# A seven-product pair at the end of the last unit of two feed-forward phases

## The chip, the core and the metric

The kernel runs on one core of one Trainium2 chip. The core has a matrix engine (TensorE, PE in the profile), whose stationary operand is loaded by a separate instruction (PEld), a vector engine (DVE), a scalar engine (ACT), a general engine (POOL) and a queue that issues the DMA transfers (SP). Matrix products are summed in eight banks of PSUM, each 128 partitions by 512 float32 values; everything else lies in SBUF. The metric is the device time of one execution in microseconds (us), the median of several runs; lower is better.

## The reference, cut to what matters

Two post-norm layers over 256 tokens of width 2048, each a mixer followed by a SwiGLU feed-forward with 5632 hidden channels:

```python
def swiglu(x, w_gate, w_up, w_down):
    return (jax.nn.silu(x @ w_gate) * (x @ w_up)) @ w_down

    for layer in range(DEPTH):
        ...
        x = layer_norm(DN_ALPHA * x + y, ln_mix_g[layer], ln_mix_b[layer])
        f = swiglu(x, ffn_w_gate[layer], ffn_w_up[layer], ffn_w_down[layer])
        x = layer_norm(DN_ALPHA * x + f, ln_ffn_g[layer], ln_ffn_b[layer])
```

The change lies in `x @ w_gate` and `x @ w_up`, in both layers. Inputs and weights are float32.

## The kernel before

**Products.** A float32 product is made of three matmuls: each operand is split into a rounded high part and the rest, and `mm3` (line 289) adds low x high, high x high and high x low into one PSUM bank. The left operand, 128 tokens by 128 channels, is the stationary one; a weight piece of 128 x 512 streams. Weights come from memory as float32, so every piece that arrives is split first: ACT copies the high part (line 127), DVE subtracts (line 128). A "half" is a transfer of two such pieces into `raw` (`load_half`, line 144, 128 x 1024 in float32, four buffers), split into `whi` and `wlo` (four buffers each in these phases), and it feeds two pieces x two token tiles x three = 12 matmuls.

**Units.** The hidden width is cut into 11 chunks of 512, which `PHASES` (line 67) groups as 3, 4 and 4. In the second and third phase each chunk is one `unit` (line 455). A unit makes four sums, gate and up for both token tiles: `c11` and `c21` are gate, `c12` and `c22` are up. The 16 slices of 128 input channels are taken as eight pairs, in an order that `PAIRS_FIRST`, `PAIRS` or `PAIRS_LAST` gives for the first, the middle and the last unit of a phase. A **plain pair** is two halves: 2 x 2 x 2 products of three matmuls, 24 matmuls. A **seven pair** treats the 2 x 2 blocks (two token tiles and two channel slices, gate and up) by a Winograd scheme with seven products instead of eight: 21 matmuls. Pairs 5, 6 and 7 (`SEVEN`) may be taken so; for them `forms_of` (line 405) makes four combinations of the activations per pair, once for each layer, ahead of the second phase and for all three pairs.

A seven pair's weights come by `load_seven` (line 433): one transfer of 1 MB into `rs`, which has a single buffer; DVE forms four sums of weights `z` (lines 445 to 447, a single buffer too), and seven pieces are split in two goes into `sh` and `sl` (two buffers each): the first three straight from `rs` (lines 444 and 448), the other four from `z` (lines 127 and 128). The seven products of a pair run in this order, each named with the bank it adds to:

```python
SEVEN_ORDER = ((0, "11", "p1"), (5, "f", "p6"), (3, "e", "p5"), (4, "g", "p7"),
               (1, "12", "c11"), (2, "h", "c12"), (6, "22", "c21"))
```

So four further banks, p1, p6, p5 and p7, collect products over a unit's seven pairs. With the four c banks they fill all eight: c on one side (`aside` or `bside` in the profile), p on the other, and the sides swap after every unit. A p bank is opened at a unit's first seven pair and closed by its last.

**The end of a unit** (lines 483 to 501). ACT copies p1 (line 485); DVE forms w, v and x from p6, p5 and p7 (lines 486 to 489), adds w to c21, subtracts v and x from c12 and c22, adds p1 to c11 (490 to 495); ACT takes the SiLU twice (491, 494) and DVE multiplies gate by up (499). Two transposes on PE for each unit (`transpose4`, line 270), one per token tile, are put off by the list `later`, until two and three halves of what comes next have been issued; ACT and DVE then split their result into `yTh` and `yTl`, the left operand of the down projection.

**The end of a phase** (lines 567 to 581). The down projection of the phase's four chunks follows its last unit: four output blocks `n`, each of eight halves, two for each chunk in order, so that the last chunk's `yT` is first read by the seventh half. Its sums start in the banks that held p1 and p6 of the last unit. After the third phase the banks are dealt out anew, as `acc`, `tr` and `mx` (`open_banks("uses")`), over the same memory.

**Order.** The program is not run in the order of this text: a scheduler places the instructions of every engine by priority and by a simulated timeline, and each engine, and SP's queue, then works its list in that order. Weight loads have priority 400, a unit's end 1000. A unit's last products may thus stand among the first products of the next unit.

Of the kernel before, what the change touches and what calls it, by code (L numbers as in the profile page):

```python
# [71 lines left out]
SEVEN = (5, 6, 7)  # L72
# [8 lines left out]
def trunk(ctx: ExitStack, tc: tile.TileContext, a, out):  # L81
# [9 lines left out]
    def open_banks(kind):  # L91

        if banks:
            banks["stack"].close()
        stack = ctx.enter_context(ExitStack())
        pool = stack.enter_context(tc.tile_pool(name="ps", bufs=1, space=PSUM, reuse_waits="tile"))
        banks.update(stack=stack, pool=pool, kind=kind, side=0)
# [16 lines left out]
    def acc():  # L114
        return bank("acc", 3) if banks["kind"] == "uses" else side_bank()
# [4 lines left out]
    def mxp():  # L120
        return bank("mx", 3)
# [15 lines left out]
    def open_ring(pool, bufs):  # L137

        rings.append((pool, bufs))
        turn[0] = -12  # L140
# [37 lines left out]
    def two(k):  # L178
        return k, k + 1
# [72 lines left out]
    def new_xT():  # L252
        xh = [ap_.tile([P, KT, P], F32R, tag=f"xTh{t}", name=f"xTh{t}") for t in range(NT)]
        xl = [ap_.tile([P, KT, P], F32R, tag=f"xTl{t}", name=f"xTl{t}") for t in range(NT)]
        return xh, xl

    def new_yT():
        yh = ap_.tile([P, 4, T], F32R, tag="yTh", name="yTh", bufs=4)
        yl = ap_.tile([P, 4, T], F32R, tag="yTl", name="yTl", bufs=4)
        return yh, yl  # L260

    def x_lhs(xT):
        return lambda tok, k: (xT[0][tok][:, k, :], xT[1][tok][:, k, :])
# [10 lines left out]
    def transpose4(src, hi, lo, ahead_by=0):  # L274
        t = trp()
        for k in range(4):
            transpose(t[:, k * P : (k + 1) * P], src[:, k * P : (k + 1) * P], ident)
        v = t.rearrange("p (k t) -> p k t", k=4)
        with tc.high_priority(offset=ahead_by):
            split(hi, lo, v)  # L280
# [19 lines left out]
    def new_stats():  # L300
        return [sm.tile([P, 4, 6], F32, tag=f"st{t}", name=f"st{t}", bufs=1) for t in range(NT)]
# [79 lines left out]
    def load_gb(pool, i, which):  # L381
        g = pool.tile([P, D], F32, tag="gam", name="gam", bufs=1)
        b = pool.tile([P, D], F32, tag="bet", name="bet", bufs=1)
        nc.sync.dma_start(g, a[f"ln_{which}_g"][i : i + 1, :].to_broadcast([P, D]))
        nc.sync.dma_start(b, a[f"ln_{which}_b"][i : i + 1, :].to_broadcast([P, D]))
        bT = pool.tile([P, 64], F32, tag="betT", name="betT", bufs=1)[:, :KT]
        nc.sync.dma_start(bT, a[f"ln_{which}_bT"][i])
        return g, b, bT
# [20 lines left out]
    def forms_of(sp, xT, out):  # L409

        n = len(SEVEN)
        xs = sp.tile([P, NT, 2 * n, P], F32, tag="rs", name="xs", bufs=1)
        fs = sp.tile([P, 4, n, P], F32, tag="z", name="fs", bufs=1)
        yield
        for t in range(NT):
            s = slice(2 * SEVEN[0], 2 * SEVEN[0] + 2 * n)
            nc.vector.tensor_tensor(xs[:, t], xT[0][t][:, s, :].bitcast(F32), xT[1][t][:, s, :].bitcast(F32), op=add)
            yield
        x11, x12, x21, x22 = (xs[:, t, e : 2 * n : 2, :] for t in range(2) for e in range(2))
        e, f, g, h = (fs[:, i] for i in range(4))  # L420
        nc.vector.tensor_tensor(e, x22, x21, op=sub)
        nc.vector.tensor_tensor(f, e, x11, op=add)
        yield
        nc.vector.tensor_tensor(g, x11, x21, op=sub)
        nc.vector.tensor_tensor(h, x12, f, op=sub)
        yield
        hi, lo = split_tile(sp, [P, 4, n, P], fs, "fm")
        for i, p in enumerate(SEVEN):
            x = lambda t, k: (xT[0][t][:, k, :], xT[1][t][:, k, :])
            e, f, g, h = (at((hi, lo), slice(None), j, i) for j in range(4))  # L430
            out[p] = {"11": x(0, 2 * p), "12": x(0, 2 * p + 1), "22": x(1, 2 * p + 1), "e": e, "f": f, "g": g, "h": h}
# [71 lines left out]
    def ffn(layer, xT, res, mix_pool, close_mix, keep, last):  # L503
        lhs = x_lhs(xT)
        w = a[f"gu{layer}"]

        def whole(c, pool, first):

            gouts = [acc() for _ in range(NT)]
            sil = {}  # L510

            def silu(tok):
                sil[tok] = pool.tile([P, NCH], F32, tag="sil", name="sil", bufs=3)
                nc.scalar.activation(sil[tok], gouts[tok], AF.Silu)

            mm_chunk([(w[c, i][:, :2], (2 * i, 2 * i + 1)) for i in range(8)], lhs, gouts, tok_major=first, after=silu)

            uouts = [mxp() for _ in range(NT)]
            y = new_yT()

            def gated(tok):
                with tc.high_priority(offset=1000):
                    nc.vector.tensor_tensor(sil[tok], sil[tok], uouts[tok], op=mult)
                s = slice(tok * P, (tok + 1) * P)
                later.append([(2 if c == PHASES[0][-1] else 4) + tok, lambda: transpose4(sil[tok], y[0][:, :, s], y[1][:, :, s])])

            mm_chunk([(w[c, i][:, 2:], (2 * i + 1, 2 * i)) for i in range(8)], lhs, uouts, after=gated)
            return y

        stack = ExitStack()  # L530
        forms, making = {}, []

        def make():
            with tc.issue_after(low[-1]):
                if next(making[0], "end") is None:
                    later.append([3, make])

        nxt = cdp = None
        groups = {}
        for pi, chunks in enumerate(PHASES):  # L540
            end = pi == len(PHASES) - 1
            for c in chunks:
                if pi == 0:
                    groups[c] = whole(c, mix_pool, c == 0)
                else:
                    groups[c] = new_yT()
                    pairs = PAIRS_FIRST if c == chunks[0] else PAIRS_LAST if c == chunks[-1] else PAIRS
                    sevens = SEVEN[:-1] if c == chunks[-1] else SEVEN
                    unit(sp, pairs, sevens, w[c], lhs, forms, groups[c], c == chunks[0])
            if pi == 0:  # L550
                close_mix()
                sp = later_pool(stack, f"sp{layer}")
                open_banks("sides")
                making.append(forms_of(sp, xT, forms))
                later.append([2, make])
            gl = [groups[c] for c in chunks]
            if end:
                stack.close()
                open_banks("uses")
                cdp = None if last else keep("cdc")  # L560
                open_ring(keep(f"er{layer}"), 4)
                open_ring(later_pool(stack, f"e{layer}"), 3)
                fp = later_pool(stack, f"g{layer}")
                nxt = None if last else new_xT()
            stats = new_stats()
            evac, norm = residual_tools(res, None, None, None, stats)
            for n in range(4):
                if cdp and n == 1:
                    consts.extend(cd_constants(cdp))
                if end and n == 1:  # L570
                    evac, norm = residual_tools(res, *load_gb(fp, layer, "ffn"), stats)
                outs = [acc() for _ in range(NT)]
                halves = [(a[f"down{layer}"][n, 2 * c + i], two(4 * ci + 2 * i)) for ci, c in enumerate(chunks) for i in range(2)]

                def after(tok):
                    with tc.high_priority(offset=1000 if end and n == 3 else 0):
                        evac(tok, n, outs[tok], pi == 0, end)
                        if end and n == 3:
                            norm(tok, nxt, out if last else None)

                mm_chunk(halves, y_lhs(gl), outs, tok_major=(end and n == 3), after=after)
            if not end:
                banks["side"] ^= 1
        if end:
            rings.pop()
            stack.close()
        return nxt
# [428 lines left out]
    def later_pool(stack, name):  # L1016
        return stack.enter_context(tc.tile_pool(name=name, bufs=1, reuse_waits="tile"))
# [4 lines left out]
    def keep(name):  # L1022
        return later_pool(kept, name)
# [136 lines left out]
```

## Time and profile before

| | |
|---|---|
| median of 3 runs | 2192.04 us (2191.01 to 2192.64) |
| the profiled execution | 2190.72 us, span of its instructions 2188.9 us |
| granted TensorE clock, mean | 0.998 |
| busy: PE, PEld, DVE, ACT | 2170.7, 1804.7, 1558.8 and 1051.3 us |
| matmuls and transposes on PE | 10048 |

The first layer's second and third phase lie between about 655 and 1230 us of the span, the second layer's between about 1603 and 2181 us. A busy PE is not by itself PE at its peak, since a matmul's record is longer than the distance to the next one: the distance of two starts is the measure used here. Times in tables are counted from the first instruction of the span.

### The profile page before, as it was taken

The page shows a single profiled execution, that of the slowest core. Times are in us where ns is not written, and L with a number is a line of the kernel's source. Part 1 is how long each engine was busy: PE and PEld are TensorE (multiplying, and loading weights), DVE is VectorE, ACT ScalarE, POOL GpSimd, SP SyncE. Part 2 cuts the span into 40 slices and gives each one's busy share as a digit, 9 for nine tenths or more (in the row PEclk, how much of TensorE's full clock was granted, in tenths as well). Part 3 has the DMA queues.
Part 4 walks back from the last instruction along what each step waited for, and adds up shares of the span by engine and source line. Part 5 has one row for each costly group of instructions (what it writes and reads, how often), then busy time and mean ns, then how long its engine had stood idle before and what let it go on. Part 6 is the DMA issues. An engine that isn't in the chain of part 4 may idle for free.

```text
span 2188.9 us, 26626 instructions
## 1 busy us (share of the span) xinstructions
PE 2170.7 (99%) x10048; PEld 1804.7 (82%) x10048; DVE 1558.8 (71%) x1954; ACT 1051.3 (48%) x1278; POOL 51.7 (2%) x51
## 2 busy tenths in 40 slices
PE   9999999999999999999999999999999999999997
PEld 7888888888888888888888888888888888888886
DVE  6886688577537787577876776667367896768765
ACT  6445544545435455444545554455344554445442
POOL 0000000000000000000000300000000000000000
PEclk9999999999999999999999999999999999999999
DMA  8555546584736565565549553747456555655563
GB/s 294 161 164 180 167 132 190 195 287 138 237 125 219 188 208 189 189 230 185 199 157 305 165 190 106 235 150 253 143 187 232 185 187 188 222 173 200 172 238 122
DMA packets 112850, 420.64 MB, mean 192 GB/s; under 512 B 13776, under 2 KB 16848, under 8 KB 105808
## 3 DMA queue, kind: packets, MB, share of 16 engines
q1 hardware_dynamic: 112720, 418.93, 57.8%
q8 instruction: 79, 1.29, 0.2%
q14 instruction: 51, 0.42, 0.1%
HBM read 416.78 MB, written 2.10 MB: 191 GB/s over the span
## 4 chain that ended last, share of the span: by engine, by line
PE 96%; DMA 1%; DVE 1%; ACT 0%; issue 0%; SPq 0%; DVEq 0%; ACTq 0%
PE acc L292 41%; PE bside L292 23%; PE aside L292 21%; PE mx L292 7%; PE mx L729 1%; PE tr L124 1%; DMA raw<-in_down 1%; DVE wlo L128 0%; DMA rs<-in_gu 0%; PE mx L775 0%; DMA raw<-in_ab_in 0%; PE bside L124 0%; PE aside L124 0%; PE mx L985 0%; ACT whi L127 0%
## 5 line engine op out<-in xcount | busy, mean ns | idle before, releaser
L128 DVE TENSOR_TENSOR wlo<-raw,whi 128x1024 fp32r<-128x1024 f32 (+1 forms) x673 | 817.8, 1224 | 438.2 <-ACT whi L127 431.2
L127 ACT CAST whi<-raw 128x1024 fp32r<-128x1024 f32 (+1 forms) x673 | 703.7, 1052 | 820.5 <-PE acc L292 262.3
L292 PE MATMUL acc<-whi,xTl 128*128 128x512 f32 x864 | 342.8, 397 | 4.8 <-ACT whi L127 4.8
L292 PE MATMUL acc<-whi,xTh 128*128 128x512 f32 x864 | 340.0, 393 | 0.0
L292 PE MATMUL acc<-wlo,xTh 128*128 128x512 f32 x864 | 337.9, 393 | 0.1
L292 PE MATMUL acc<-whi,yTl 128*128 128x512 f32 x512 | 200.8, 392 | 0.2
L292 PE MATMUL acc<-whi,yTh 128*128 128x512 f32 x512 | 199.6, 390 | 0.0
L292 PE MATMUL acc<-wlo,yTh 128*128 128x512 f32 x512 | 197.7, 390 | 0.0
L292 PEld LDWEIGHTS acc<-whi,xTl 128*128 128x128 f32 x864 | 162.9, 189 | 37.2 <-ACT whi L127 5.7
L292 PEld LDWEIGHTS acc<-wlo,xTh 128*128 128x128 f32 x864 | 162.9, 189 | 33.9 <-DVE wlo L128 1.1
L292 PEld LDWEIGHTS acc<-whi,xTh 128*128 128x128 f32 x864 | 163.1, 189 | 31.1
L292 PE MATMUL bside<-whi,xTl 128*128 128x512 f32 x336 | 131.4, 391 | 0.7 <-ACT g L485 0.6
L292 PE MATMUL bside<-whi,xTh 128*128 128x512 f32 x336 | 131.0, 390 | 0.0
L292 PE MATMUL aside<-whi,xTl 128*128 128x512 f32 x336 | 131.0, 390 | 0.0
L292 PE MATMUL aside<-whi,xTh 128*128 128x512 f32 x336 | 130.9, 390 | 0.0
L292 PE MATMUL bside<-wlo,xTh 128*128 128x512 f32 x336 | 128.1, 390 | 0.0
L292 PE MATMUL aside<-wlo,xTh 128*128 128x512 f32 x336 | 128.1, 390 | 0.0
L292 PEld LDWEIGHTS acc<-wlo,yTh 128*128 128x128 f32 x512 | 96.1, 188 | 20.6 <-DVE wlo L128 0.5
L292 PEld LDWEIGHTS acc<-whi,yTl 128*128 128x128 f32 x512 | 96.2, 188 | 20.0 <-DVE res L310 0.5
L292 PEld LDWEIGHTS acc<-whi,yTh 128*128 128x128 f32 x512 | 96.2, 188 | 19.4
L128 DVE TENSOR_TENSOR sl<-z,sh 128x2048 fp32r<-128x2048 f32 x44 | 100.7, 2289 | 6.4 <-ACT sh L127 5.7
L292 PE MATMUL bside<-whi,yTl 128*128 128x512 f32 x256 | 99.8, 390 | 0.0
(266 smaller groups left out, 3414.3 us busy)
## 6 DMA issues: line engine op xcount, KB each, us to landing
raw<-in_gu SPq DMA_DIRECT2D x264, 512.0 KB, 4.7
raw<-in_down SPq DMA_DIRECT2D x176, 512.0 KB, 3.9
raw<-in_ab_in SPq DMA_DIRECT2D x127, 512.0 KB, 4.2
rs<-in_gu SPq DMA_DIRECT2D x44, 1024.0 KB, 5.9
raw<-in_cd_in SPq DMA_DIRECT2D x40, 512.0 KB, 4.2
raw<-in_ab_out SPq DMA_DIRECT2D x32, 512.0 KB, 4.4
raw<-in_cd_out SPq DMA_DIRECT2D x32, 512.0 KB, 4.2
bias<-in_na_bias SPq DMA_DIRECT2D x32, 64.0 KB, 4.2
```

Source lines behind the costliest of these rows:

```text
L124: return nc.tensor.transpose(o, src, eye)
L127: nc.scalar.copy(hi, src)
L128: return nc.vector.tensor_tensor(lo, src, hi.bitcast(F32), op=sub).ins
L292: ins = nc.tensor.matmul(o, lhs[a], rhs[b], start=start and n == 0, stop=stop and n == 2)
L729: nc.tensor.matmul(m[:, 2 * h + s, :], kk[:, h, s * P : (s + 1) * P], qq[:, h, r * P : (r + 1) * P], start=True, stop=True,)
```

## The change

In each phase's last unit, `sevens` was `SEVEN[:-1]`: pairs 5 and 6 were seven pairs, and pair 7, which is the last in `PAIRS_LAST`, was a plain one. Now pair 7 is a seven pair there too. `PAIRS_LAST` itself, (0, 1, 5, 2, 6, 3, 4, 7), stays. Four units are affected, the last of the second and of the third phase in each of the two layers.

```diff
--- before
+++ after
@@ -545,7 +545,7 @@
                 else:
                     groups[c] = new_yT()
                     pairs = PAIRS_FIRST if c == chunks[0] else PAIRS_LAST if c == chunks[-1] else PAIRS
-                    sevens = SEVEN[:-1] if c == chunks[-1] else SEVEN
+                    sevens = SEVEN
                     unit(sp, pairs, sevens, w[c], lhs, forms, groups[c], c == chunks[0])
```

In `unit`, the following is what the pair then runs through, on the first branch instead of the second:

```python
            if p in sevens:
                ...
                wt = load_seven(sp, w[p], behind.pop(0))
                for i, x, name in SEVEN_ORDER:
                    product(name, forms[p][x], wt(i))
            else:
                for n, ks in ((0, (2 * p, 2 * p + 1)), (1, (2 * p + 1, 2 * p))):
                    hi, lo = load_half(w[p][:, 2 * n : 2 * n + 2])
                    ...
                    half_done()
```

## The prediction, made before the changed kernel was run

> **What bounds the kernel now.** I read the page first: busy times, granted clock, and the chain that ended last.
>
> ```profile
> span 2188.9 us, 26626 instructions
> PE 2170.7 (99%) x10048; PEld 1804.7 (82%) x10048; DVE 1558.8 (71%) x1954; ACT 1051.3 (48%) x1278; POOL 51.7 (2%) x51
> ...
> PEclk9999999999999999999999999999999999999999
> ...
> PE 96%; DMA 1%; DVE 1%; ACT 0%; issue 0%; SPq 0%; DVEq 0%; ACTq 0%
> ```
>
> The chain is PE for 96% of the span, at an unthrottled clock. Whether PE has any slack is told by the distance of its matmuls, not by its busy time. So next the chain in order of time, where rows say how long so many matmuls in a row took, and then the table of PE's own waits.
>
> ```profile
> 734.42 2.72 PE aside L292 x12
> ...
> 891.34 77.12 PE bside L292 x340
> ...
> 1119.81 4.13 PE aside L292 x18
> ```
>
> ```profile
> PE acc L292 <- ACT whi L127: 4.8, 1, 4.8
> PE mx L292 <- DVE ptl L128: 1.2, 1, 1.2
> PE bside L292 <- ACT g L485: 0.6, 1, 0.6
> ```
>
> A down projection's 340 matmuls take 77.12 / 340 = 0.2268 us each, a plain half 2.72 / 12 = 0.227, and the 18 of a seven pair 4.13 / 18 = 0.229, a row that holds the start behind a transpose. So a seven pair's matmuls cost what others do. PE waited three times that the trace can name, 6.6 us in all, and 4.8 of these lie ahead of the first matmul. In the stages that the change touches PE simply runs its list: what leaves the list is time won, unless a new wait comes.
>
> **The change part by part.** *Removed on PE.* Pair 7 goes from 24 matmuls to 21, three fewer in each of four units: 12 x 0.2268 = 2.72 us. The transposes, the evacuation's instructions and the number of banks stay the same. There are as many weight loads on PE as matmuls (the x10048 twice), so they fall alike.
>
> *Added on DVE and ACT.* Two halves' splits go, one seven pair's preparation comes. Their rows, from the groups of instructions with shapes kept apart (the last figure ahead of the second bar is the mean in ns):
>
> ```profile
> L128 DVE TENSOR_TENSOR wlo<-raw,whi 128x1024 fp32r<-128x1024 f32 x671 | 816.4, 1226 | 437.0 <-ACT whi L127 430.0 <-PE acc L292 2.4 <-DMA raw<-in_ab_in 1.3
> L127 ACT CAST whi<-raw 128x1024 fp32r<-128x1024 f32 x671 | 702.5, 1053 | 819.3 <-PE acc L292 262.3 <-PE bside L292 169.7 <-PE aside L292 144.1
> L128 DVE TENSOR_TENSOR sl<-z,sh 128x2048 fp32r<-128x2048 f32 x44 | 100.7, 2289 | 6.4 <-ACT sh L127 5.7
> L127 ACT CAST sh<-z 128x2048 fp32r<-128x2048 f32 x44 | 84.2, 1914 | 21.1 <-DVE z L447 20.8
> L448 DVE TENSOR_TENSOR sl<-rs,sh 128x1536 fp32r<-128x1536 f32 x44 | 77.2, 1754 | 27.8 <-ACT sh L444 27.8
> L444 ACT CAST sh<-rs 128x1536 fp32r<-128x1536 f32 x44 | 65.3, 1484 | 70.6 <-DMA rs<-in_gu 32.0 <-PE bside L292 19.9 <-PE aside L292 18.6
> L445 DVE TENSOR_TENSOR z<-rs 128x1024 f32<-128x1024 f32 x44 | 53.8, 1222 | 31.3 <-DMA rs<-in_gu 31.2
> L446 DVE TENSOR_TENSOR z<-z,rs 128x512 f32<-128x512 f32 x44 | 30.2, 686 | 0.3
> L447 DVE TENSOR_TENSOR z<-z,rs 128x512 f32<-128x512 f32 x44 | 30.1, 685 | 0.1
> ```
>
> DVE: 1.222 + 0.686 + 0.685 + 1.754 + 2.289 = 6.64 us against 2 x 1.226 = 2.45, so 4.18 us more in each unit. ACT: 1.484 + 1.914 = 3.40 against 2.11, so 1.29 more. Is there room? The busy times in two stretches of 23 us around the last unit of the first layer's third phase (columns: PE, PEld, DVE, ACT, POOL, clock, DMA share):
>
> ```profile
> 1094.00:1117.00 23.00, 23.00 (x105) 19.04 (x104) 22.90 (x24) 13.59 (x14) 0.00 (x0) 1.00 0.46 159
> 1117.00:1140.00 23.00, 23.00 (x105) 19.04 (x104) 13.88 (x17) 7.84 (x10) 0.00 (x0) 1.00 0.43 143
> ```
>
> Ahead of 1117 us, where the unit before is evacuated and two seven pairs are prepared, DVE has no room at all. From 1117 to 1140 it has 9.1 us free, and pair 7 asks for 4.2. This is where its weights would be made, so I cost DVE and ACT at nothing; without that cover the price would be up to 4.18 us a unit, 16.7 in all.
>
> *When pair 7's weights are ready.* They can't be loaded before pair 6 has left the one `rs` buffer. The order in time, by engines, and the row of the load in the table of DMA issues (the last figure is the median from issue to landing):
>
> ```profile
> 1096.29 0.33 SPq L443 DMA_DIRECT2D rs<-in_gu  x1
> ...
> 1110.74 0.68 DVE L447 TENSOR_TENSOR z<-z,rs 128x512 f32<-128x512 f32 x1
> ...
> 1114.81 2.28 DVE L128 TENSOR_TENSOR sl<-z,sh 128x2048 fp32r<-128x2048 f32 x1
> ...
> 1139.64 0.39 PE L292 MATMUL acc<-whi,yTl 128*128 128x512 f32 x1
> ...
> 1145.09 0.60 PE L124 MATMUL tr<-ident,g 128*128 128x128 f32 x4
> ```
>
> ```profile
> rs<-in_gu SPq DMA_DIRECT2D x44, 1024.0 KB, 5.9
> ```
>
> Pair 6's load was issued at 1096.29, its last use of `rs` ended at 1111.42, its last split at 1117.09: 20.8 us from issue to ready, on that full DVE. The down projection begins at 1139.64, so the plain pair 7 begins 24 x 0.2268 = 5.44 us earlier, at 1134.20, and the seven pair would begin there too. From 1111.42, at pair 6's slow pace, its weights are ready at 1132.2, 2.0 us early; its own work of 6.64 us on DVE and 1.91 on ACT behind 5.9 us of transfer gives 1126, 8 us early. Either way nothing waits, so I take zero.
>
> *Moved: the unit's end.* Before, the p banks closed with pair 6 and were combined long before the end; now they close inside the last pair, as in the middle units. Those show what this costs. Unit 10 (the last) follows unit 9:
>
> ```profile
> 1094.27 0.57 ACT L485 COPY g<-bside 128x512 f32<-128x512 f32 x1
> ...
> 1122.62 0.59 ACT L485 COPY g<-aside 128x512 f32<-128x512 f32 x1 [2.19 <-PE aside L292]
> ```
>
> ```profile
> 1097.28 0.68 DVE L486 TENSOR_TENSOR g<-g,bside 128x512 f32<-128x512 f32 x1
> ...
> 1106.07 0.68 DVE L499 TENSOR_TENSOR g<-g,u 128x512 f32<-128x512 f32 x1
> ...
> 1113.61 0.68 DVE L499 TENSOR_TENSOR g<-g,u 128x512 f32<-128x512 f32 x1
> ```
>
> In unit 9 p6's bank is read by 1097.96, 3.7 us after p1's copy began; the gated products start 11.8 and 19.3 us after it. In unit 10 the copy stood 17 us ahead of the down projection. With a seven pair last, p1 closes 18 matmuls (4.1 us) ahead of the unit's end, which itself comes 0.68 us earlier, at 1138.96; the copy starts at about 1135.1. At unit 9's pace p6 is free at 1138.8, and the down projection's second token tile, which takes that bank, begins six matmuls after 1138.96, at 1140.3: no wait. The products then start at 1146.9 and 1154.4. The transposes stand at 1145.1 today and may slide back: `yT` is first read by the seventh half, 6 x 2.72 = 16.3 us after the unit's end, at 1155.3 (first tile) and 1157.6 (second, with the transposes' 0.9 in between). 1154.4 plus product, transposes and splits (0.7 + 0.5 + 1.3) is 1156.9. So even unit 9's pace, with DVE full, just covers it; behind the last unit there are no more seven pairs to prepare, so the real margin is larger. I take zero here too, with the rivals' price as the other end.
>
> *DMA.* One transfer of 1 MB takes the place of two of 512 KB on the same queue: no bytes more.
>
> **Sum.** 2190.72 (profiled execution, its span 2188.9 and 1.8 around it) - 2.72 = 2188.0. The median of the three runs is 1.32 us above that execution, so on the median 2192.04 - 2.72 = **2189.3 us**, 0.12% less.
>
> **The rivals.** *Handovers that stall, gain partly or wholly lost.* The kernel has twelve handovers with a seven pair last, and one of them, in the second layer, shows a wait:
>
> ```profile
> 2035.18 7.23 DMA rs<-in_gu
> ```
>
> ```profile
> 2042.43 1.49 ACT L444 CAST sh<-rs 128x1536 fp32r<-128x1536 f32 x1 [4.25 <-DMA rs<-in_gu]
> 2043.82 1.04 ACT L127 CAST whi<-raw 128x1024 fp32r<-128x1024 f32 x1
> 2044.77 0.57 ACT L485 COPY g<-bside 128x512 f32<-128x512 f32 x1
> ```
>
> ```profile
> 2044.37 0.39 PE L292 MATMUL aside<-sl,xTh 128*128 128x512 f32 x1
> 2045.39 0.50 PE L292 MATMUL bside<-whi,xTl 128*128 128x512 f32 x1 [0.63 <-ACT g L485]
> ...
> 2052.10 0.49 PE L292 MATMUL bside<-sl,xTh 128*128 128x512 f32 x1
> 2052.70 0.50 PE L292 MATMUL bside<-whi,xTl 128*128 128x512 f32 x1
> ```
>
> A load landed late, ACT stood in front of it, and p1's copy stood behind that on ACT: PE's next matmul came 1.02 us after the one before instead of 0.23, and a second gap in the same unit took 0.60 instead of 0.23: 1.16 us lost. The Trainium skill ("TensorE: Matmul & The Clock Gate", the section on the array's architectural detail) says that ScalarE and VectorE take their queues strictly first in, first out; the trace agrees, ready copy behind unready cast. The four new handovers have no seven load behind them but down halves, so such a wait is less likely, yet p1's copy, now late, stands among their casts. One to four times 1.16 us: 2190.5 to 2194.0.
>
> *Slower: pair 7's weights come late.* Place: SP works its list in order, and pair 7's load stands among the halves of pairs 3, 4 and the down projection. Point: at the slow pace of 20.8 us it decides when the load is issued after 1134.2 - 20.8 = 1113.4, only 2.0 us after `rs` comes free; at the fast one (about 14.5) after 1119.7. Issued at, say, 1118.3 with a full DVE, it is 4.9 us late; in four units 19.6 - 2.7, so 2209. For it: the one buffer, and DVE full till 1117. Against: 9.1 us of free DVE behind that, and a list whose simulated times have held in nearly all the handovers. The same skill page (the part on the HAM clock gate) has PE at half clock after an idle window of about 3.4 us; no run here shows it, the granted clock being 1.00 beside waits of about 1 us. By it each such wait would cost an estimated 1.7 us more, 2216.
>
> *More is won.* The wait at 2044 us is a late transfer, and everything behind the second phase moves earlier by 0.7 to 2 us. If it goes, 2.72 + 1.2, and with a scrap elsewhere 4.4: 2187.6.
>
> **How the numbers follow.** Differences under about 0.2% (4.4 us) can't be told from none on this kernel. The forecast has 0.62, stalled handovers 0.18, late weights 0.12, a larger gain 0.08. Forecast and stalls lie within 0.2%: same 0.80, faster 0.08, slower 0.12. The range, 2187.3 to 2194.5, takes in the first two, part of the last, and the spread of runs (0.8 us either way).
>
> **What would show it.** Right: 10036 PE instructions, no new wait of PE between the units' ends and the down projections, `sl` of a twelfth seven pair in each of the four phases ready before its first product, and steps of 0.227 us. Wrong: PE waiting for `sh`, `sl` or line 485 at one of the four ends, the load of `rs` issued after 1114 us in the first layer, or transposes of `g` delaying PE. A reordering by the scheduler of work far from these places would also break the sum.

## The result and the profile after

The changed kernel takes 2197.71 us (median of 7 runs, 2194.97 to 2200.62) against 2192.04 us before: 5.7 us or 0.26% **slower**, ratio 1.0026 with a 95% interval of 1.0017 to 1.0035. The profiled execution took 2194.97 us, the shortest of the seven, with a span of 2192.9 us. The lines of its page that answer to those shown of before:

```profile
span 2192.9 us, 26600 instructions
PE 2169.8 (99%) x10036; PEld 1803.8 (82%) x10036; DVE 1574.2 (72%) x1966; ACT 1055.9 (48%) x1278; POOL 52.4 (2%) x51
...
PE 97%; DVE 1%; DMA 1%; issue 0%; ACT 0%; SPq 0%; DVEq 0%; ACTq 0%
```

The twelve matmuls are gone (10036 for 10048), and yet the span is 4.0 us longer. PE's own waits, by releaser, say where to look (total, times, longest):

```profile
PE acc L292 <- DVE u L489: 5.3, 2, 2.7
PE acc L292 <- ACT whi L127: 4.8, 1, 4.8
PE mx L292 <- DVE ptl L128: 1.3, 1, 1.3
```

The last two rows were there before, all but unchanged. The first is new: twice PE stood still for 2.7 us, at the first matmul into an `acc` bank, until line 489 on DVE (x = w + p5) was done. In order of time, PE at the end of the first layer's third phase:

```profile
1136.51 0.84 PE L292 MATMUL aside<-sl,fmh 128*128 128x512 f32 x3
1137.19 0.39 PE L292 MATMUL bside<-sl,fmh 128*128 128x512 f32 x1
1137.42 0.39 PE L292 MATMUL bside<-sh,xTl 128*128 128x512 f32 x1
1137.65 0.39 PE L292 MATMUL bside<-sh,xTh 128*128 128x512 f32 x1
1137.87 0.39 PE L292 MATMUL bside<-sl,xTh 128*128 128x512 f32 x1
1140.93 0.50 PE L292 MATMUL acc<-whi,yTl 128*128 128x512 f32 x1 [2.67 <-DVE u L489]
```

and DVE over the same time:

```profile
1129.62 2.29 DVE L128 TENSOR_TENSOR sl<-z,sh 128x2048 fp32r<-128x2048 f32 x1
...
1137.01 0.69 DVE L486 TENSOR_TENSOR g<-g,aside 128x512 f32<-128x512 f32 x1 [1.34 <-PE aside L292]
1137.80 0.69 DVE L487 TENSOR_TENSOR u<-g,aside 128x512 f32<-128x512 f32 x1
1138.41 0.68 DVE L490 TENSOR_TENSOR g<-g,bside 128x512 f32<-128x512 f32 x1
1139.01 0.68 DVE L488 TENSOR_TENSOR g<-g,aside 128x512 f32<-128x512 f32 x1
1139.60 0.68 DVE L492 TENSOR_TENSOR u<-bside,u 128x512 f32<-128x512 f32 x1
1140.20 0.67 DVE L489 TENSOR_TENSOR u<-g,aside 128x512 f32<-128x512 f32 x1
```

The unit's last matmul starts at 1137.87 and the down projection's first at 1140.93: 3.06 us instead of 0.23, so 2.83 lost, and the same again at the end of the second layer's third phase. In the kernel before, line 489 had ended at 1129.20, and the down projection began at 1139.64, 10.4 us later and right behind the unit's last matmul:

```profile
1128.51 0.69 DVE L489 TENSOR_TENSOR u<-g,aside 128x512 f32<-128x512 f32 x1
...
1139.42 0.39 PE L292 MATMUL bside<-wlo,xTh 128*128 128x512 f32 x1
```

Three things add up to the wait. The first bank that the down projection takes is the one that p5 had (line 489 is p5's last reader, and releases it). Line 489 is the sixth in a row of DVE instructions that start when p6 is closed. And p6, p5 and p7 are closed only by the three matmuls at 1136.51, a mere 1.4 us ahead of the unit's last start, although their operand `sl` had been ready since 1131.91.

At the end of the second phase line 489 is just as late (its end is 884.06, the down projection begins at 881.27), and PE doesn't wait:

```profile
881.05 0.39 PE L292 MATMUL aside<-sl,xTh 128*128 128x512 f32 x1
881.27 0.39 PE L292 MATMUL bside<-whi,yTl 128*128 128x512 f32 x1
```

```profile
883.38 0.68 DVE L489 TENSOR_TENSOR u<-g,bside 128x512 f32<-128x512 f32 x1
```

There the first banks are those of p1 and p6. The numbers of the banks in the built program of the changed kernel bear this out for both phases, in the first layer:

```
second phase, last unit:  p1 7, p6 6, p5 5, p7 4    down projection: first sums in 7 and 6
third phase, last unit:   p1 1, p6 2, p5 0, p7 3    down projection: first sums in 0 and 2
```

In the second phase the banks go on within one pool, and the first sums took the banks of p1 and p6, which are read first. After the third phase a new pool is laid over them and begins with bank 0, whoever had it; in the kernel before, too, that was p5, only its last reader was done early enough. The description of the kernel further up, that the down projection starts in the banks of p1 and p6, holds for the second phase alone.

The sum for the profiled execution: -2.72 for the matmuls, + 2 x 2.83 for the waits = +2.94, and about 1.7 for one stretch at half clock right after the second wait, of which more in the last section: +4.6, against +4.25 measured from profiled execution to profiled execution. The stretch shows in four us behind that wait (the last three figures are the granted clock, the DMA share and GB/s):

```profile
2092.00:2096.00 4.00, 4.00 (x12) 3.15 (x11) 2.04 (x4) 0.63 (x1) 0.00 (x0) 0.57 0.01 4
```

### The profile page after: what moved, and what is told of

Read it like the earlier page. It is cut to its first block, busy times and chain, and to the rows that moved or that the text cites. A ratio compares the mean times of both kernels' runs of the same rounds, so it can differ in the third digit from the quotient of the medians.

```text
span 2192.9 us, 26600 instructions
## 1 busy us (share of the span) xinstructions
PE 2169.8 (99%) x10036; PEld 1803.8 (82%) x10036; DVE 1574.2 (72%) x1966; ACT 1055.9 (48%) x1278; POOL 52.4 (2%) x51
## 4 chain that ended last, share of the span: by engine, by line
PE 97%; DVE 1%; DMA 1%; issue 0%; ACT 0%; SPq 0%; DVEq 0%; ACTq 0%
PE acc L292 43%; PE bside L292 23%; PE aside L292 21%; PE mx L292 7%; PE mx L729 1%; PE tr L124 1%; DMA rs<-in_gu 0%; PE mx L775 0%; PE bside L124 0%; PE aside L124 0%; PE mx L985 0%; DMA raw<-in_ab_in 0%; PE mx L124 0%; DVE wlo L128 0%; DVE res L329 0%
## 5 line engine op out<-in xcount | busy, mean ns | idle before, releaser
L128 DVE TENSOR_TENSOR wlo<-raw,whi 128x1024 fp32r<-128x1024 f32 (+1 forms) x665 | 806.6, 1223 | 432.8 <-ACT whi L127 427.8
L127 ACT CAST whi<-raw 128x1024 fp32r<-128x1024 f32 (+1 forms) x665 | 695.4, 1051 | 800.5 <-PE acc L292 262.1
L292 PE MATMUL bside<-whi,xTl 128*128 128x512 f32 x320 | 124.8, 390 | 0.1
L292 PE MATMUL aside<-whi,xTl 128*128 128x512 f32 x320 | 124.8, 390 | 0.0
L292 PE MATMUL aside<-whi,xTh 128*128 128x512 f32 x320 | 124.7, 390 | 0.0
L292 PE MATMUL bside<-whi,xTh 128*128 128x512 f32 x320 | 124.7, 390 | 0.0
L292 PE MATMUL bside<-wlo,xTh 128*128 128x512 f32 x320 | 121.9, 390 | 0.0
L292 PE MATMUL aside<-wlo,xTh 128*128 128x512 f32 x320 | 121.9, 390 | 0.0
L128 DVE TENSOR_TENSOR sl<-z,sh 128x2048 fp32r<-128x2048 f32 x48 | 109.9, 2289 | 7.0 <-ACT sh L127 6.1
L448 DVE TENSOR_TENSOR sl<-rs,sh 128x1536 fp32r<-128x1536 f32 x48 | 84.2, 1754 | 32.2 <-ACT sh L444 32.2
```

What stands on the lines that cost most here:

```text
L127: nc.scalar.copy(hi, src)
L128: return nc.vector.tensor_tensor(lo, src, hi.bitcast(F32), op=sub).ins
L292: ins = nc.tensor.matmul(o, lhs[a], rhs[b], start=start and n == 0, stop=stop and n == 2)
L448: nc.vector.tensor_tensor(lo[:, :3], raw[:, :3], hi[:, :3].bitcast(F32), op=sub)
```

## The experiments

All were run beside the kernel before, whose medians in the three series were 2192.19, 2191.92 and 2192.48 us. "Theory" is that the loss is PE's wait for line 489, by the bank; the rivals are late weights of pair 7, and costs spread by the scheduler's new lists.

**The second phase's ends alone.**

```diff
-                    sevens = SEVEN
+                    sevens = SEVEN[:-1] if end and c == chunks[-1] else SEVEN
```

> Pair 7 is a seven pair in the last unit of the second phase only, in both layers; the third phase is as before. Theory (the bank): the loss is PE's wait for line 489, the last reader of p5's bank, which only the third phase's down projection takes first; then nothing waits here, six matmuls go, and the time is 1.36 us below before (2190.7 where before is 2192.0). Rival (late weights): pair 7's weights or the late closing of the p banks hold PE up at every end, so this kernel too waits 1 to 3 us at its two ends and is 1 to 4 us above before. Rival (the list): the scheduler's other order of work costs time far from the ends; then this kernel differs from before by an amount that no wait at its ends explains.

Measured: 2190.53 us, ratio 0.9995 (0.9986 to 1.0003), 1.7 us below before at a forecast of 1.36; no wait of PE at any of the four ends, no row for line 489. The interval takes in no change, so the gain by itself isn't established; that nothing is lost at these ends is. Late weights fall: the same pair, prepared in the same way, costs nothing here.

**The third phase's ends alone.**

```diff
-                    sevens = SEVEN
+                    sevens = SEVEN[:-1] if c == chunks[-1] and not end else SEVEN
```

> Pair 7 is a seven pair in the last unit of the third phase only, in both layers. Theory (the bank): both gaps of 3.06 us between two matmuls, ended by line 489, are there as in the changed kernel; 2 x 2.83 - 1.36 = 4.3 us above before, and 1.7 us more for each stretch of 3.4 us at clock 0.5 that follows a gap, so 4.3 to 7.7 above. Rival (late weights): about half of the changed kernel's loss, 2 to 3 us above before. Rival (the list): no relation to the changed kernel's loss.

Measured: 2199.38 us, ratio 1.0035 (1.0022 to 1.0049), 7.2 us above before. PE's waits hold the row of the changed kernel:

```profile
PE acc L292 <- DVE u L489: 5.3, 2, 2.7
```

So the whole loss sits at the two ends of the third phase. Its profiled execution had no stretch at half clock, and took 2197.75 us: the forecast's range, 4.3 to 7.7 us above before, was met, but not by way of the half clock alone (more below the table).

**One operand changed at line 489**, in all units: v is w + p5 already, so x = v + p7 is the same sum, and p5 is last read by line 487.

```diff
-            nc.vector.tensor_tensor(x, w_, b["p5"], op=add)
+            nc.vector.tensor_tensor(x, v, b["p7"], op=add)
```

> The changed kernel, with line 489 written as x = v + p7 instead of w + p5: the same sum in another order, after which p5's bank is last read by line 487, three DVE instructions earlier. Theory (the bank): the two gaps of 3.06 us shrink to under 0.6 us, no stretch at clock 0.5 follows, and the time is 2 to 2.7 us below before (2189.3 to 2190.0). Rival (late weights): pair 7's products close as late as they did, so most of the gaps stay, and the time is 3 us or more above before. Rival (the list): a new order, time anywhere.

Measured: 2188.63 us, ratio 0.9985 (0.9976 to 0.9994), 3.6 us below before and 9.1 below the changed kernel. Not a row of PE's waits is at a unit's end any more; what is left there stands at handovers between units, for p1's copy:

```profile
PE bside L292 <- ACT g L485: 1.0, 2, 0.6
PE aside L292 <- ACT g L485: 0.9, 2, 0.6
```

In this build the list changed too: p1 now has bank 0. So the run shows that the wait is the loss, not yet through which of the two, reader or bank, it went.

**Pairs 4 and 7 exchanged**, so that a plain pair follows the last seven pair:

```diff
-PAIRS_LAST = (0, 1, 5, 2, 6, 3, 4, 7)
+PAIRS_LAST = (0, 1, 5, 2, 6, 3, 7, 4)
```

> The changed kernel, with pairs 4 and 7 exchanged in the order of a phase's last unit, so that the third seven pair is followed by a plain one. Theory (the bank): the p banks close 24 matmuls (5.4 us) further ahead of the down projection, line 489 ends ahead of it, no gap is left, and the time is 2.7 us below before (2189.3). Rival (late weights): pair 7's weights are needed 5.4 us earlier than in the changed kernel, so a wait shows in front of its products, and the time is above before by 1 to 6 us. Rival (the list): a new order, time anywhere.

Measured: 2202.59 us, ratio 1.0050 (1.0038 to 1.0063), 10.4 us above before. Here the theory's number failed, and taught the most. The waits for line 489 grew to 4.47 us from start to start. PE's list, and DVE's:

```profile
1136.82 0.84 PE L292 MATMUL aside<-sl,fmh 128*128 128x512 f32 x3
```

```profile
1130.60 2.29 DVE L128 TENSOR_TENSOR sl<-z,sh 128x2048 fp32r<-128x2048 f32 x1
...
1137.32 0.69 DVE L486 TENSOR_TENSOR g<-g,aside 128x512 f32<-128x512 f32 x1 [3.29 <-PE aside L292]
1137.93 1.23 DVE L128 TENSOR_TENSOR wlo<-raw,whi 128x1024 fp32r<-128x1024 f32 x1
...
1141.46 1.22 DVE L128 TENSOR_TENSOR wlo<-raw,whi 128x1024 fp32r<-128x1024 f32 x1
1142.59 0.68 DVE L489 TENSOR_TENSOR u<-g,aside 128x512 f32<-128x512 f32 x1
```

Pair 7 comes earlier in the text, its `sl` is ready at 1132.89, and still its three closing matmuls stand at 1136.82, with only six of pair 4's 24 behind them; two splits of down weights now lie within DVE's row. Where a pair stands in the text doesn't settle when the list closes its banks. Late weights are no better off: they are ready 3.9 us ahead of the matmuls that use them.

**Pair 7's matmuls kept in the order of the text**, each product's three together, in a phase's last unit:

```diff
-    def unit(sp, pairs, sevens, w, lhs, forms, yT, opening):
+    def unit(sp, pairs, sevens, w, lhs, forms, yT, opening, pinned=None):
...
-        def product(name, x, wt):
+        def product(name, x, wt, pin=False):
...
-            mm3(b[name], x, wt, name not in begun, left[name] == 0)
+            mm3(b[name], x, wt, name not in begun, left[name] == 0, pin)
...
-                    product(name, forms[p][x], wt(i))
+                    product(name, forms[p][x], wt(i), p == pinned)
...
-                    unit(sp, pairs, sevens, w[c], lhs, forms, groups[c], c == chunks[0])
+                    unit(sp, pairs, sevens, w[c], lhs, forms, groups[c], c == chunks[0], 7 if c == chunks[-1] else None)
```

> The changed kernel, with the 21 matmuls of pair 7 in a phase's last unit kept in the order of the text, so that each product's three stand together. In the changed kernel the closing matmuls of p6, p5 and p7 stand 1.4 to 0.9 us ahead of the unit's last start, although their operand had been ready for 4.6 us. Theory (the list closes them late): p6 now closes 3.4 us and p7 2.0 us ahead of the end, line 489 follows some 2 us earlier than before, the gaps of 3.06 us fall to about 1 us or less, nothing runs at clock 0.5, and the time is 1 to 2.7 us below before. Rival (the order on DVE alone): the list on DVE keeps line 489 where it was, the gaps stay over 2 us, and the time stays 3 us or more above before.

Measured: 2192.53 us, ratio 1.0003 (0.9994 to 1.0012). The time missed the forecast of 1 to 2.7 us below before. The waits from start to start fell to 1.63 us, by 1.4, not by 2. DVE, and PE:

```profile
1135.42 1.23 DVE L128 TENSOR_TENSOR wlo<-raw,whi 128x1024 fp32r<-128x1024 f32 x1 [0.27 <-ACT whi L127]
1136.56 0.68 DVE L486 TENSOR_TENSOR g<-g,aside 128x512 f32<-128x512 f32 x1
...
1139.75 0.68 DVE L489 TENSOR_TENSOR u<-g,aside 128x512 f32<-128x512 f32 x1
```

```profile
1138.85 0.39 PE L292 MATMUL bside<-sl,xTh 128*128 128x512 f32 x1
1140.48 0.50 PE L292 MATMUL acc<-whi,yTl 128*128 128x512 f32 x1 [1.25 <-DVE u L489]
```

Line 486 now starts 2.29 us ahead of the unit's last matmul, instead of 0.86, and no longer waits for PE. It moved by 1.43 us, though p6's closing matmul moved by 2.04 (to 3.40 us ahead of the last): a split of down weights now stands in front of it on DVE. So the late closing is about half of the wait; what is left goes with DVE's row of six instructions up to line 489, whose order no run changed by itself.

**Another bank first**: an `mx` bank asked for and not used as the banks are dealt out anew, so that the first sum falls to bank 3, which p7 had. It is last read by line 488.

```diff
                 open_banks("uses")
+                mxp()
```

> The changed kernel, with one mx bank asked for (and not used) as the banks are dealt out anew after the third phase, so that the first sum of the down projection falls to the bank of p7, not of p5. p7 is last read by line 488, two DVE instructions (1.2 us) ahead of line 489. Theory (which bank is first sets the wait): the two gaps go from 3.06 to about 1.9 us, ended by line 488, no stretch at clock 0.5, time 0.5 us above to 0.5 us below before. Rival (the unit's whole end is late, whatever the bank): gaps as in the changed kernel, 3 us or more above before.

Measured: 2193.56 us, ratio 1.0008 (0.9999 to 1.0017), 1.6 us above before, where 0.5 at most was forecast. The wait is 1.87 us from start to start, and its releaser is now line 488:

```profile
1140.27 0.39 PE L292 MATMUL bside<-sl,xTh 128*128 128x512 f32 x1
1142.14 0.50 PE L292 MATMUL acc<-whi,yTl 128*128 128x512 f32 x1 [1.48 <-DVE g L488]
```

Nothing but the banks was changed, and the wait moved by just the two DVE instructions between the two readers: the bank sets it.

**One operand changed, in the third phase's last unit only.**

```diff
-    def unit(sp, pairs, sevens, w, lhs, forms, yT, opening):
+    def unit(sp, pairs, sevens, w, lhs, forms, yT, opening, closing=False):
...
-            nc.vector.tensor_tensor(x, w_, b["p5"], op=add)
+            nc.vector.tensor_tensor(x, *((v, b["p7"]) if closing else (w_, b["p5"])), op=add)
...
-                    unit(sp, pairs, sevens, w[c], lhs, forms, groups[c], c == chunks[0])
+                    unit(sp, pairs, sevens, w[c], lhs, forms, groups[c], c == chunks[0], end and c == chunks[-1])
```

> The changed kernel with x = v + p7 at line 489 in the last unit of the third phase only; all other units as in the changed kernel. Theory (the bank): no gap over 0.6 us at the ends; without the four waits of 0.6 to 0.75 us for line 485 that the version with x = v + p7 in all units shows, the time is 2.7 us below before or a little better than that version. Rival (that version's gain came from another order of its list): the gaps of 3.06 us come back in part, and the time is above before.

Measured: 2190.28 us, ratio 0.9990 (0.9981 to 0.9999). The banks are those of the changed kernel here, and only the reader differs:

```profile
1138.94 0.39 PE L292 MATMUL bside<-sl,xTh 128*128 128x512 f32 x1
1139.61 0.50 PE L292 MATMUL acc<-whi,yTl 128*128 128x512 f32 x1 [0.28 <-DVE u L487]
```

0.67 us from start to start, released by line 487, as the bank theory has it. The time came out 1.6 us below before, not 2.7, and not below the version with the line in all units; 0.9 of the difference is what is left of the two waits.

**The changed kernel again.**

> The changed kernel as it is, beside the other three. Theory: two gaps of 3.06 us; a stretch of 3.4 us at clock 0.5 follows one of them or both, as the free-running phase of the throttle falls, so 2.9 us above before without any, 4.6 with one, 6.3 with two.

Measured: 2198.06 us, ratio 1.0025 (1.0015 to 1.0035). Its profiled execution has both waits, and a stretch at half clock behind each.

**The line alone, and once more with the change**: the kernel before with x = v + p7 in all units, beside the changed kernel with it.

> The kernel before (pair 7 plain in the last units), with x = v + p7 at line 489 in all units. Theory (the bank): there is no wait for line 489 in the kernel before, so the line itself brings nothing: within 1 us of before. Rival (the line pays by itself): 1 us or more below before, which would explain why the changed kernel with this line in all units came out 1.7 us below the one with it in two units.

> The changed kernel with x = v + p7 in all units once more, beside the kernel before with the same line. Theory: 12 matmuls fewer and no wait at the ends, so 2.7 us below before, and 2.7 us below the other kernel of this pair; the four waits of 0.6 to 0.75 us for line 485 may come back or not, 0 to 2.8 us.

Measured: the kernel before with the line 2191.83 us, ratio 0.9995 (0.9986 to 1.0004), so the line alone brings nothing that can be told; the changed kernel with it 2188.16 us, ratio 0.9981 (0.9973 to 0.9990), 4.3 us below before and 3.7 below the other. This is the version that **beats both kernels**, twice, by 3.6 and 4.3 us. The matmuls explain 2.7 of that; about one us stays open. The waits for line 485 between units don't explain it by these profiles: they were 1.9 to 2.0 us in total with this version against 0.6 in the kernel before. Beside the other kernel of this pair they do fit: it had 3.3 us of them, so 1.3 more, and 2.7 + 1.3 = 4.0 stands against the measured 3.7.

The series together. "Wait" is the distance of the two starts at each of the two ends of the third phase; "worked out" is -0.227 for each matmul gone, plus the waits less 0.227 each:

| kernel | wait, us | worked out, us | measured against before, us |
|---|---|---|---|
| second phase alone | none | -1.4 | -1.7 |
| third phase alone | 3.06 | +4.3 | +7.2 |
| changed; again | 3.06 | +2.9 | +5.7; +6.1 |
| pairs 4 and 7 exchanged | 4.47 | +5.8 | +10.4 |
| pair 7 in the order of the text | 1.63 | +0.1 | +0.6 |
| another bank first | 1.87 | +0.6 | +1.6 |
| x = v + p7, last units | 0.67 | -1.8 | -1.6 |
| x = v + p7, all units; again | none | -2.7 | -3.6; -4.3 |

Where the wait stays under 2 us the sum meets the measurement within about 1 us, but for the last row's 1.6. Where it is 3 us or more, 3 to 5 us are missing. The half clock, in the last section, is a part of that and not the whole. The profiled execution of the third phase alone had none of it, and its span is still 7.1 us above that of before, with 4.3 worked out. Of the 2.8 us between, 1.5 lie in single steps of PE at the handovers between units, which cost 2.7 us there and 1.2 in the kernel before; 1.3 stay open. Such steps differ between executions of one program (0.8 us and 2.1 in the two profiled ones of the changed kernel), so they need not be a cost of the scheduler's new list; the runs don't exclude that rival for them.

## Why the prediction was wrong, point by point

- **What bounds the kernel, and the 2.72 us**: right. PE runs its list end to end, the three matmuls in each unit went, and where no wait came in their place the time fell (second phase alone; x = v + p7).
- **Room on DVE and ACT for pair 7's preparation**: right in its conclusion. The same stretches of 23 us, after:

```profile
1094.00:1117.00 23.00, 23.00 (x106) 19.02 (x105) 22.90 (x25) 12.75 (x12) 0.00 (x0) 1.00 0.53 192
1117.00:1140.00 23.00, 21.26 (x96) 17.27 (x94) 16.21 (x17) 9.21 (x9) 0.00 (x0) 1.00 0.44 151
```

  The preparation found its place, with 6.8 us of DVE to spare.
- **When pair 7's weights are ready**: on time, at 1131.91, by the slow pace rather than the fast. What held them was neither of the two things weighed there (the `rs` buffer, DVE) but ACT, which waited on PE twice in a row, ahead of a cast of `whi` and then ahead of the first `sh`:

```profile
1124.70 1.05 ACT L127 CAST whi<-raw 128x1024 fp32r<-128x1024 f32 x1 [5.13 <-PE bside L292]
1126.29 1.48 ACT L444 CAST sh<-rs 128x1536 fp32r<-128x1536 f32 x1 [0.53 <-PE aside L292]
```

- **"Moved: the unit's end" is the step that failed**: it took the wait at zero, and that wait measured 2.83 us at each of the third phase's two ends. Two of its parts were wrong. It looked at p6's bank for the second token tile, which did take it, and left the first tile to p1's. That holds within a pool (second phase) and not across the new pool (third phase), where the first tile took p5's bank, and the runs with another bank and another reader moved the wait accordingly. And "p1 closes 18 matmuls (4.1 us) ahead" took the seven products in the order of the text. p1 was copied a little ahead of the forecast 1135.1:

```profile
1134.45 0.59 ACT L485 COPY g<-aside 128x512 f32<-128x512 f32 x1
```

  But p6, p5 and p7 closed together, 1.4 us ahead of the end, and the row of DVE instructions could only begin there. Even so p6's bank was free at 1137.70, ahead of the forecast 1138.8; it was p5's that was asked for. Pinning the order took 1.4 us off the wait.
- **The pace taken over from unit 9** (3.7 us from p1's copy to p6's release) was the right stretch read for the wrong bank. In the kernel before, p5's release in unit 9 ends at 1106.15, 11.9 us after p1's copy:

```profile
1105.47 0.68 DVE L489 TENSOR_TENSOR u<-g,bside 128x512 f32<-128x512 f32 x1
```

  Held against the forecast copy at 1135.1, that row alone would have put p5's bank far behind the down projection's start, had its reader been asked for.
- **"Differences under about 0.2% (4.4 us) can't be told from none"** was too wide: the intervals reach 0.08% to 0.14% to either side, and differences of 0.15% and 0.19% (x = v + p7) were told.
- **Rivals**: "handovers that stall" had the right kind of event, a bank not yet free, but took its place from line 485 on ACT and its price of 1.16 us from there; it was 2.83 us, and certain rather than a matter of late transfers. "Late weights" didn't happen. The half clock, given no weight of its own, came in.

## What to carry to other kernels

When work is moved to the end of a stage, ask not only when it is done but which buffer the next stage takes first and who reads that buffer last; across a pool that is dealt out anew, the answer isn't the order in which buffers come free. Where a scheduler writes the lists, the order of the text doesn't say when a sum is closed: read it from a stage that ends in the same way, for every reader, not for the first alone. A reader can often be chosen: the same sum, taken from another intermediate, released the bank early and turned a loss of 6 us into a gain of about 4.

## What the runs showed of the hardware

A wait of under 3 us was followed by a stretch of half clock in some executions and not in others. The changed kernel's second run, in the stretches around its two waits (columns: PE, PEld, DVE, ACT, POOL, granted clock, DMA share):

```profile
1139.00:1142.60 3.60, 1.20 (x6) 0.66 (x4) 3.50 (x6) 0.63 (x1) 0.00 (x0) 1.00 0.58 218
1142.60:1146.00 3.40, 3.13 (x7) 2.51 (x8) 2.71 (x5) 0.63 (x1) 0.00 (x0) 0.50 0.00 0
2091.00:2094.90 3.90, 1.49 (x7) 0.91 (x5) 3.56 (x6) 0.63 (x1) 0.00 (x0) 1.00 0.55 212
2094.90:2098.30 3.40, 3.14 (x7) 2.49 (x8) 2.70 (x5) 0.63 (x1) 0.00 (x0) 0.50 0.02 5
```

At clock 0.50 for 3.4 us, 7 matmuls start where 15 would: about 1.7 us lost by each stretch. In that run's series the two executions with a mean clock of 0.998 took 2196.5 and 2196.6 us, the seven with 0.996 or 0.997 took 2197.9 to 2198.6. Among the profiled executions with a wait of 3.06 us, the clock halved behind one of two waits (changed kernel), behind none of two (third phase alone) and behind both (changed kernel again); with waits of 4.47 us behind both; with waits of 1.9 us or less behind none of them (pair 7 in the order of the text, another bank, x = v + p7 in the last units). So a wait of 3 us costs 2.8 us or 4.5 us, and a part of what is missing in the table, though not all of it, is this. The Trainium skill ("TensorE: Matmul & The Clock Gate", part 1, on the HAM clock gate) has the clock halve after an idle window of about 3.4 us that runs freely; the free phase agrees with a halving in some executions only, but here 2.7 us without a matmul were enough, behind three of six such waits.
